# RWKV-7 layer of a hybrid decoder step: triangular inverses from transposed blocks by columns, samples' loads a pair ahead, masks and the second group's norm on VectorE, another gate for the first output half

## The chip, the cores and the metric

The kernel runs on one core of a Trainium2 chip. The metric is device time in microseconds (us), the time of one execution. In the profile PE is TensorE (matmul), PEld its weight loads, DVE VectorE, ACT ScalarE, POOL GpSimd and SP SyncE, which here only issues DMAs; ACT issues the loads of the weights beside its own work. Each engine works through its own instructions in order and waits at the first one whose operands or buffers are not ready.

## The reference, cut to what matters

One step of a two-layer decoder: 16 meta tokens and 512 prompt tokens, and 8 samples of 4 tokens each. Layer 0 is a gated DeltaNet mixer and a convolutional FFN, layer 1 an RWKV-7 mixer (16 heads of 64) and another FFN. All that follows concerns the RWKV mixer. Its core is a recurrence over tokens for each head:

```python
def rwkv_step(S, xs):
    r_t, w_t, k_t, v_t, kk_t, a_t = xs
    sa = jnp.einsum('bhvk,bhk->bhv', S, kk_t)
    S = (S * w_t[:, :, None, :] - sa[..., None] * (kk_t * a_t)[:, :, None, :]
         + v_t[..., None] * k_t[:, :, None, :])
    y = jnp.einsum('bhvk,bhk->bhv', S, r_t)
    return S, y
...
    kk = l2norm(heads(k * k_k))
...
    S, y = lax.scan(rwkv_step, S0.astype(F32), (tm(rh), tm(dh), tm(kh), tm(vh), tm(kk), tm(ah)))
    y = jnp.moveaxis(y, 0, 1)
    mu = jnp.mean(y, axis=-1, keepdims=True)
    var = jnp.mean(jnp.square(y - mu), axis=-1, keepdims=True)
    y = ((y - mu) * lax.rsqrt(var + GN_EPS)).reshape(B, L, D) * ln_w.astype(F32) + ln_b.astype(F32)
    bonus = jnp.sum(rh * kh * r_k.astype(F32), axis=-1, keepdims=True) * vh
    y = y + bonus.reshape(B, L, D)
    out = (y * gate.astype(F32)).astype(h.dtype) @ wo
```

The prompt's scan starts from zero states, the samples' from the given `state_rwkv_S`. Outputs are the activations and the new states.

## The kernel before, in words

All 560 tokens (32 of the samples, 16 meta, 512 of the prompt) lie along the free axis, features on the partitions. Every dense product in fp32 is made of three fp32r products: a weight tile is split into `hi` (on ACT, L70) and `lo` (on DVE, L71), the activations likewise, and `dense_g` (L115) runs hi·hi, hi·lo and lo·hi, two column halves each: 48 matmuls for a weight tile of 8 contraction blocks.

The scan is done in chunks: chunk 0 holds the samples and the meta tokens (48 columns), chunks 1 to 8 hold 64 prompt tokens each. Heads go in two groups G = 0, 1 of 8 heads, four pairs each. The steps for a group are generators that a small planner, `Weave`, interleaves: its `slots` hold the dense products of k, r and v, then the second group's `products2`, `gates` and `out_half`, in this order; its `chains` hold the others. A chain yields (PE cost, latency, banks), and the planner goes to whichever chain is due on its virtual clock, otherwise to the next dense matmuls. A slot may have a gate, a condition that must hold before it starts. The framework then schedules the instructions of each engine from a model of their times. The chains are:

- `sums` (L1298 and on): squares of k per head and token, their reciprocals `ssq` (upper partitions), the negatives `nw`.
- `early(G)` (from L1382): for each chunk the strictly triangular product of keys, `pa` in PSUM (L1392), times a mask on DVE (L1396) into an SBUF tile `L` of ring `s` (two buffers, shared with others); then eight ACT operations, one for each head, scale the rows by `ssq` (L1398); `to_inverse` stores the diagonal blocks (32 x 32; 16 x 16 for chunk 0) to DRAM on SP (L1373, L1378).
- `inverse0(G)` and `inverse(G)` load these blocks, one to a partition, into the tile `X` (24 partitions of 16 x 16 and 128 of 32 x 32), and `tri_inplace` inverts them in place on DVE, row by row from the last: a product (L1023) into the scratch tile `tri`, written across its rows, and a sum (L1025). The result goes to DRAM and from there into the chunks' tiles `A` (XX, A and A58 by name in the profile). Group 0's inverse runs beside the dense products of r and v, group 1's beside group 0's recurrence.
- `products(G, c)` (L1353, masks L1360): all key and query products of a chunk, whose corner blocks the inverses replace.
- `merge(G, q)` (L1439 to L1449): from the two inverted diagonal blocks of two chunks to the full 64 x 64 inverse. Four merges a group, one after the other.
- `ktokens`, `vtokens`: transposed keys and values by way of DRAM.
- `rec(G)` (L1594 to L1652): the serial chain over chunks. A chunk is four groups of matmuls, L1624 and L1628, L1633, L1642, L1651, each waiting for an evacuation of the one before. `load(c + 2)` on SP (L1572, L1573) fetches keys and values two chunks ahead. Group 1 starts when group 0 ends.
- `outnorm` (L1671 to L1691): the norm of two chunks' outputs: sum and mean on DVE, eight ACT operations that shift the heads (L1674), ACT square, DVE sum, inverse root in small DVE operations (L351 to L356), eight ACT operations that scale (L1681), four transpositions on PE (L1685), then gate and bonus on DVE (L1690, L1691).
- `samples(G)` (L1705 to L1761), four head pairs one after the other, sharing one set of buffers: `load(p)` issues 10 DMAs on SP (the states as block diagonals `S0b`, L1716 to L1717; `S0`, L1718; tokens, L1719 to L1724) and POOL places the queries in `z`; ten matmuls (L1738, L1739), two (L1744), two (L1749), on ACT eight masked copies `vm` (L1754), a matmul (L1757), and the new state through DVE (L1758) and POOL (L1759) to a store (L1760). When all four are done the samples have their own `outnorm`.
- `gates` (L1547): gate projection; `out_half` (from L1779): the first half, by contraction, of the output projection for all 8 output tiles (weights `w_o`, activations `osA`, built in a buffer that group 0's samples used), each stored to DRAM as `x2`. It starts when group 0's six norms and the gates are done and a merge of group 1 has been noted.

After the planner has run, the second half (`osB`) follows, adding `x2` (L1813), and then the FFN of layer 1.

## Time and profile before

| what | us |
|---|---|
| median of 3 runs (1908.01 to 1916.1) | 1912.06 |
| the profiled execution's own time | 1913.3 |
| its span in the profile | 1911.3 |
| PE busy / DVE busy / ACT busy / POOL busy | 1801.1 / 1154.5 / 803.9 / 369.0 |

The page of the profile gives the busy time of each engine, the clock that TensorE was granted in 40 slices (PEclk, in tenths of full speed), and the costliest groups of instructions: line, engine, operation, output <- input, count, then busy time, mean ns of one, and the idle time of the engine before them with what ended it. The view by windows gives the same for chosen stretches. A timeline row has start, length, engine, line, and in brackets the idle time just before with its releaser. The RWKV mixer runs from about 870 to 1480 us of the span. PE is busy for all 120 us between 1020 and 1140, where DVE is busy for 98.90; in 1190 to 1230 PE is busy for 28.55 of 40 us.

### The profile page before, as it was taken

The numbers are of one execution on the slowest core, as the hardware profiler recorded it, in microseconds if no ns is written. First come the engines' busy times: TensorE is split into PE (matmuls) and PEld (weight loads), VectorE is DVE, ScalarE is ACT, GpSimd is POOL, SyncE is SP. The second block draws the span as 40 slices with busy tenths as digits, with TensorE's granted clock in tenths as the row PEclk, the third lists the DMA queues.
The fourth block names the chain that finished last, engine by engine and source line by source line (L and its number), as shares of the span: only waits on it lengthen the run. The fifth ranks groups of instructions, "written<-read, shape, count | busy, mean of one in ns | idle before, by whom it ended". The sixth has DMA issues, their size and how long they took to land.

```text
span 1911.3 us, 36670 instructions
## 1 busy us (share of the span) xinstructions
PE 1801.1 (94%) x14673; PEld 1718.5 (90%) x14673; DVE 1154.5 (60%) x2221; ACT 803.9 (42%) x1779; POOL 369.0 (19%) x616
## 2 busy tenths in 40 slices
PE   7999999999999999998989999799997999999996
PEld 6889998789999999998778997788786999999996
DVE  6698973875555553337787977874555555554223
ACT  4766434442222222222976535554644322222221
POOL 3442403621222220013110000021001111111011
PEclk9999998999999999999898999896898999999998
DMA  4233232433222223444122244332235322223331
GB/s 131 76 91 93 70 90 104 150 122 120 82 89 89 80 87 104 120 155 98 48 70 62 70 117 121 98 91 80 78 102 163 123 89 89 89 88 91 99 109 67
DMA packets 128010, 186.13 MB, mean 97 GB/s; under 512 B 63088, under 2 KB 75376, under 8 KB 127840
## 3 DMA queue, kind: packets, MB, share of 16 engines
q10 hardware_dynamic: 34448, 111.63, 18.7%
q1 hardware_dynamic: 93392, 72.17, 13.0%
q8 instruction: 116, 1.90, 0.4%
q14 instruction: 54, 0.44, 0.1%
HBM read 151.56 MB, written 32.18 MB: 96 GB/s over the span
## 4 chain that ended last, share of the span: by engine, by line
PE 76%; DVE 12%; ACT 3%; DMA 3%; issue 1%; POOL 0%; SPq 0%; DVEq 0%; ACTq 0%
PE pd L115 56%; PE pd L138 3%; PE pg L1353 1%; DVE lo L71 1%; PE pg L1739 1%; PE pg L1628 1%; DVE it L425 1%; PE pg L1624 1%; PE pg L1651 1%; PE pg L1642 1%; DVE tri L1023 1%; PE pg L835 1%; PE pg L1633 1%; DVE cv L593 1%; DMA xd<-xo 1%
## 5 line engine op out<-in xcount | busy, mean ns | idle before, releaser
L115 PE MATMUL pd<-x,hi 128*128 128x280 f32 (+7 forms) x4768 | 837.5, 297 | 23.5 <-ACT hi L70 9.1
L115 PEld LDWEIGHTS pd<-x,hi 128*128 128x128 f32 (+1 forms) x4768 | 695.4, 192 | 30.8 <-ACT hi L70 9.3
L115 PE MATMUL pd<-x,lo 128*128 128x296 f32 (+5 forms) x2384 | 516.4, 297 | 5.6 <-DVE lo L71 5.6
L70 ACT ACTIVATE hi<-raw 128x1024 fp32r<-128x1024 f32 (+3 forms) x218 | 219.8, 1009 | 481.7 <-PE pd L115 447.4
L115 PEld LDWEIGHTS pd<-x,lo 128*128 128x128 f32 (+1 forms) x2384 | 382.9, 192 | 9.9 <-DVE lo L71 6.8
L71 DVE TENSOR_TENSOR lo<-raw,hi 128x1024 fp32r<-128x1024 f32 (+3 forms) x218 | 255.7, 1173 | 219.1 <-ACT hi L70 212.6
L218 POOL TENSOR_TENSOR s<-s,sq 128x560 f32<-128x560 f32 (+2 forms) x30 | 50.8, 1693 | 303.7 <-ACT sq L216 273.9
L304 DVE TENSOR_TENSOR gp<-pd,s 128x528 f32<-128x528 f32 (+1 forms) x44 | 30.8, 701 | 105.9 <-PE pd L115 105.9
L115 PE MATMUL pd<-hl,hi 128*128 128x280 f32 (+1 forms) x448 | 93.5, 290 | 0.0
L115 PE MATMUL pd<-hh,hi 128*128 128x280 f32 (+1 forms) x448 | 93.3, 290 | 0.0
L115 PE MATMUL pd<-hh,lo 128*128 128x280 f32 (+1 forms) x448 | 93.3, 290 | 0.0
L316 ACT ACTIVATE gs<-cv 128x528 f32<-128x528 f32 (+1 forms) x44 | 28.1, 639 | 147.3 <-DVE cv L314 147.3
L115 PE MATMUL pd<-hb,hi 128*128 128x280 f32 (+1 forms) x512 | 85.8, 290 | 0.0
L115 PEld LDWEIGHTS pd<-hb,hi 128*128 128x128 f32 x512 | 72.8, 188 | 0.0
L115 PEld LDWEIGHTS pd<-hh,lo 128*128 128x128 f32 x448 | 70.8, 188 | 0.0
L115 PEld LDWEIGHTS pd<-hh,hi 128*128 128x128 f32 x448 | 70.6, 188 | 0.0
L115 PEld LDWEIGHTS pd<-hl,hi 128*128 128x128 f32 x448 | 70.5, 188 | 0.0
L319 POOL TENSOR_TENSOR gs<-gs,s 128x560 f32<-128x560 f32 (+1 forms) x44 | 60.8, 1382 | 38.1 <-ACT gs L317 38.1
L322 DVE TENSOR_TENSOR h<-pd,gs 128x560 f32<-128x560 f32 (+1 forms) x44 | 32.1, 730 | 57.0 <-POOL gs L319 57.0
L308 POOL COPY fnew<-gp 128x2 f32<-128x2 f32 x44 | 8.1, 185 | 291.5 <-DVE gp L304 291.5
L1023 DVE TENSOR_TENSOR tri<-X 128x4 f32<-128x4 f32 (+26 forms) x124 | 56.0, 451 | 5.2 <-POOL X L1014 2.2
L138 PE MATMUL pd<-os,hi 128*128 128x280 f32 x256 | 52.8, 303 | 2.5 <-ACT os L183 1.9
(539 smaller groups left out, 3039.6 us busy)
## 6 DMA issues: line engine op xcount, KB each, us to landing
raw<-w_up ACTq DMA_DIRECT2D x88, 512.0 KB, 3.3
raw<-w_in ACTq DMA_DIRECT2D x32, 512.0 KB, 3.3
raw<-w_down ACTq DMA_DIRECT2D x32, 512.0 KB, 3.6
raw<-w_down ACTq DMA_DIRECT2D x16, 384.0 KB, 3.0
kbd<-kst SPq DMA_DIRECT2D x18, 256.0 KB, 2.0
KB<-kbd SPq DMA_DIRECT2D x18, 256.0 KB, 3.0
xd<-xo SPq DMA_DIRECT2D x16, 280.0 KB, 2.1
raw<-gdn_out ACTq DMA_DIRECT2D x8, 512.0 KB, 3.3
```

The lines of the kernel that those rows point to most:

```text
L70: nc.scalar.activation(hi[:R, :kt, :M], raw[:R, :kt, :M], AF.Copy)
L71: lo_eng.tensor_tensor(lo[:R, :kt, :M], raw[:R, :kt, :M], hi[:R, :kt, :M].bitcast(F32), op=ALU.subtract)
L115: nc.tensor.matmul(ps[b][:M, :c1 - c0] if isinstance(ps, list) else ps[:M, b, :c1 - c0], lhsT=w[:, kk, :M], rhs=x[:, c0:c1], start=(k == 0 ...
L138: nc.tensor.matmul(ps[:, b, :c1 - c0], lhsT=a, rhs=x[:, c0:c1], start=(k == i == 0), stop=(k == len(xs) - 1 and i == 2))
L218: nc.gpsimd.tensor_tensor(self.acc[:, :self.w], self.acc[:, :self.w], sq, op=ALU.add)
L304: nc.vector.tensor_tensor(two(gp[:, m0:]), pm, two(s[:, mo:mo + ml]), op=ALU.mult)
L316: nc.scalar.activation(gs[:, mo:mo + ml], cv[:, m0 - 2:], AF.Silu)
L319: nc.gpsimd.tensor_tensor(gs, gs, s[:, :n_main], op=ALU.mult)
L322: nc.vector.tensor_tensor(two(h), ps[:, :, :hw], two(gs), op=ALU.mult)
L425: nc.vector.tensor_tensor(t.rearrange("p n j -> p j n"), U[:n, i:R, c0:], L[:n, i, i:R].unsqueeze(2).to_broadcast([n, m, k]), op=ALU.mult)
L593: nc.vector.scalar_tensor_tensor(cv, gp[:, i:i + 584], cw[i], cv, op0=ALU.mult, op1=ALU.add)
L1023: nc.vector.tensor_tensor(t.rearrange("p n j -> p j n"), X[:n, i + 1:c1, c0:c1], X[:n, i, i + 1:c1].unsqueeze(2).to_broadcast([n, m1, k]), ...
```

## The change

1. `early` now computes the transposed blocks (operands of L1392 swapped, on the lower partitions, with a transposed mask `maskT` that one DMA puts into the free half of `nw`), and the eight ACT scalings of a chunk are gone. Instead `by_block(G, q)`, called from `sums`, copies the reciprocals on ACT into a tile of ring `s`, transposes them on PE, copies them on ACT and stores them to DRAM (`Dd`). `inverse` and `inverse0` load them as `D` (2 and 3 DMAs on SP) into `E.rest`, and DVE multiplies `X` by `D` once.
2. `tri_inplace` goes by columns: row j of `X` holds the block's column, the product is written along rows, the sums go down a column, and a DVE memset clears the used part of row j. For a 32 x 32 block that makes 43 products and sums and 31 memsets (before: 47 products and sums), for 16 x 16 it makes 15 and 15 (before: 15).
3. `samples`: the load is cut into three, each issued as soon as its buffers are free in the pair before. The eight ACT copies `vm` become one DVE product.
4. `outnorm` of group 1: shift and scale of the eight heads are one DVE operation each; group 0 keeps ACT's.
5. `out_half` no longer asks for a merge of group 1.

```diff
 def tri_inplace(E, X, tmp, n, R):
...
-    for i in range(R - 2, -1, -1):
-        m = R - 1 - i
-        step = min(m, N // m)
-        for c1 in range(R, i + 1, -step):
-            c0 = max(c1 - step, i + 1)
-            m1, k = c1 - i - 1, c1 - c0
-            t = tmp[:n, :m1 * k].rearrange("p (a b) -> p a b", a=k)
-            nc.vector.tensor_tensor(t.rearrange("p n j -> p j n"), X[:n, i + 1:c1, c0:c1],
-                                    X[:n, i, i + 1:c1].unsqueeze(2).to_broadcast([n, m1, k]), op=ALU.mult)
-            nc.vector.tensor_reduce(X[:n, i, c0:c1], t, axis=AX.X, op=ALU.add, negate=True)
+    for j in range(1, R):
+        i = 0
+        while i < j:
+            w = j - i
+            k = min(w, N // w)
+            t = tmp[:n, :k * w].rearrange("p (a b) -> p a b", a=k)
+            nc.vector.tensor_tensor(t, X[:n, i:i + k, i:j], X[:n, j, i:j].unsqueeze(1).to_broadcast([n, k, w]), op=ALU.mult)
+            nc.vector.tensor_reduce(X[:n, i:i + k, j], t, axis=AX.X, op=ALU.add, negate=True)
+            i += k
+        nc.vector.memset(X[:n, j, 0:j], 0.0)
         yield
...
+                by_block(m // 4, q)
                 W.chain(early(m // 4))
...
+        def by_block(G, q):
+            pt = bank([64])
+            s = E.xp.tile([P, T], F32, tag="s", name="Dt", bufs=2)
+            t = s[:72, :64]
+            nc.scalar.activation(s[up, 64:136].rearrange("p (c h) -> p c h", c=9), q, AF.Copy)
+            nc.tensor.transpose(pt[:72], s[up, 64:136], E.ident[up, up])
+            nc.scalar.activation(t, pt[:72], AF.Copy)
+            nc.sync.dma_start(out=Dd[G], in_=t)
...
-                        nc.tensor.matmul(pa[hh][up, u, :n], lhsT=KB[r, 4 * G + u, c, 1, :], rhs=KR[r, 4 * G + u, c, 1, :n], start=True, stop=True)
+                        nc.tensor.matmul(pa[hh][dn, u, :n], lhsT=KR[r, 4 * G + u, c, 1, :], rhs=KB[r, 4 * G + u, c, 1, :n], start=True, stop=True)
...
-                for h in range(8):
-                    nc.scalar.activation(L[:, h], L[:, h], AF.Copy, scale=ssq[up, c, 8 * G + h:8 * G + h + 1])
...
+            for j in range(2):
+                nc.sync.dma_start(out=D[64 * j:64 * j + 64], in_=Dd[G, 8:72, 32 * j:32 * j + 32])
+            nc.vector.tensor_tensor(X, X, D.unsqueeze(1).to_broadcast([P, 32, 32]), op=ALU.mult)
...
+            if G:
+                nc.vector.tensor_tensor(y, y, mu[r].unsqueeze(2).to_broadcast([r.stop - r.start, 8, 64]), op=ALU.add)
+            else:
+                for u in range(8):
+                    nc.scalar.activation(y[:, u], y[:, u], AF.Identity, bias=mu[r, u:u + 1])
...
-                for b8 in range(8):
-                    nc.scalar.activation(vm[:, b8], vx, AF.Copy, scale=ind[:, b8:b8 + 1])
+                nc.vector.tensor_tensor(vm, vx.unsqueeze(1).to_broadcast([P, 8, 64]), ind.unsqueeze(2).to_broadcast([P, 8, 64]), op=ALU.mult)
...
-                    [lambda: normed[0] == 6 and bool(gated) and bool(merged[1]), out_half()]]
+                    [lambda: normed[0] == 6 and bool(gated), out_half()]]
```

The loads of the samples, before and now (`load` and its three parts issue the same 10 DMAs; `load_states` also has the four POOL copies into `z`):

```diff
             for q in range(4):
                 p = 4 * G + q
-                load(p)
...
-                yield 0, 2.5, 0
...
                 nc.scalar.activation(PY, ps, AF.Copy)
+                if q < 3:
+                    load_states(p + 1)
...
                 nc.tensor.matmul(ps, lhsT=kt, rhs=vm, start=True, stop=True)
+                if q < 3:
+                    load_tokens(p + 1)
...
                 nc.sync.dma_start(out=O["rwkv_Ss"][p], in_=S0)
+                if q < 3:
+                    load_own(p + 1)
```

The change gives the planner other steps and other times, so instructions move on every engine. Two places matter for what follows. The first is DVE at the end of group 0's first large inverse (before: L1023 and L1025 its products and sums, L71 the split of a weight, 24 partitions the small inverse of group 1; L1439 is the first merge's transposition, which waits for the inverse's way through DRAM):

```order
L1023 TENSOR_TENSOR tri<-X 128x19x12
L1025 TENSOR_REDUCE X<-tri 128x12
L1023 TENSOR_TENSOR tri<-X 128x7x7
L71 TENSOR_TENSOR lo<-raw,hi 128x1024
L1025 TENSOR_REDUCE X<-tri 128x7
L71 TENSOR_TENSOR lo<-raw,hi 128x1024
L1023 TENSOR_TENSOR tri<-X 24x1
```

The same place now (L1379 is the mask of a chunk's products, L1537 to L1531 belong to `vtokens`, L1445 is the product of group 1's small blocks with D, L1462 the transposition):

```order
L1023 TENSOR_TENSOR tri<-X 128x361
L1379 TENSOR_TENSOR A<-pg,rc 128x4x128
L1024 TENSOR_REDUCE X<-tri 128x19
L1026 MEMSET X 128x31
L71 TENSOR_TENSOR lo<-raw,hi 128x1024
L1379 TENSOR_TENSOR A<-pg,rc 128x4x128
L1537 TENSOR_TENSOR H<-pg,H 128x280
L1528 TENSOR_TENSOR prod<-KR,KB 128x48
L1537 TENSOR_TENSOR H<-pg,H 128x280
L1529 TENSOR_TENSOR prod<-KR,KB 128x512
L1531 TENSOR_SCALAR brk<-rc,pv 128x128
L1445 TENSOR_TENSOR X<-X,rest 24x256
```

The inverse now ends ahead of work that stood before it: counted from the early products on, 11 weight splits stand ahead of its last row instead of 13, and 19 masks of products instead of 20. The second place is PE at the start of the first output half (before, in chunk 7 of group 1's recurrence: L1685 on XX is the norm of group 0's samples, L1744 and L1749 are steps of group 1's samples, L1642 and L1651 end chunk 7, L1624 and L1628 open chunk 8, `osA` is the output half):

```order
L1685 MATMUL pg<-cm,XX 128x32 x4
L1744 MATMUL pg<-A 32x64 x2
L1642 MATMUL pg<-KB 128x128 x4
L1651 MATMUL pg<-KB,A 64x64 x8
L115 MATMUL pd<-osA,hi 128x274 x2
L1624 MATMUL pg<-KB,KR 128x128 x4
L1628 MATMUL pg<-KB,A 64x64 x7
L1628 MATMUL pg<-KB,A 128x64
L1749 MATMUL pg<-A 32x64 x2
L115 MATMUL pd<-osA,hi 128x274 x5
```

The same now, in chunk 5 (the lines are in turn L1714, L1781, L1665, L1674, L1647, L1651 and L1786):

```order
L1714 MATMUL pg<-cm,XX 128x32 x4
L1781 MATMUL pg<-A 32x64 x2
L1665 MATMUL pg<-KB 128x128 x4
L1674 MATMUL pg<-KB,A 64x64 x6
L115 MATMUL pd<-osA,hi 128x274
L1674 MATMUL pg<-KB,A 64x64 x2
L115 MATMUL pd<-osA,hi 128x274 x5
L1647 MATMUL pg<-KB,KR 128x128 x4
L1651 MATMUL pg<-KB,A 64x64 x7
L1651 MATMUL pg<-KB,A 128x64
L1786 MATMUL pg<-A 32x64 x2
```

Both times the half comes right behind the norm of group 0's samples, but that norm now stands two chunks earlier in the recurrence, and the half's matmuls lie between the steps of chunks 5 to 8.

42 lines of the change are left out of this document (28 added, 14 removed).

## The prediction

> **What bounds the kernel now.** I read the page first: its engine table and the slices of the clock.
>
> ```profile
> span 1911.3 us, 36670 instructions
> PE 1801.1 (94%) x14673; PEld 1718.5 (90%) x14673; DVE 1154.5 (60%) x2221; ACT 803.9 (42%) x1779; POOL 369.0 (19%) x616
> PEclk9999998999999999999898999896898999999998
> ```
>
> PE is busy for 94% of the span, so only its 110 us of idle time and its time at a low clock can be won. Then I cut the RWKV layer, all that the change touches, into stretches with the view by windows (columns: length; busy time of PE, PEld, DVE, ACT, POOL; clock, DMA share, GB/s).
>
> ```profile
> 990.00:1020.00 30.00, 22.03 (x213) 20.80 (x212) 27.97 (x61) 22.49 (x70) 5.62 (x7) 0.72 0.20 49
> 1020.00:1140.00 120.00, 120.00 (x1025) 112.82 (x1024) 98.90 (x220) 55.95 (x150) 7.29 (x11) 0.99 0.32 92
> 1140.00:1190.00 50.00, 45.86 (x508) 39.90 (x507) 36.70 (x98) 27.20 (x61) 3.13 (x4) 0.90 0.48 125
> 1190.00:1230.00 40.00, 28.55 (x256) 24.31 (x254) 37.97 (x101) 21.50 (x68) 2.41 (x5) 0.87 0.26 78
> 1280.00:1300.00 20.00, 15.02 (x124) 12.86 (x123) 15.36 (x43) 15.38 (x45) 1.31 (x6) 0.91 0.31 79
> 1300.00:1340.00 40.00, 40.00 (x385) 34.73 (x382) 13.03 (x32) 18.19 (x56) 4.97 (x11) 0.57 0.27 77
> 1380.00:1400.00 20.00, 18.23 (x122) 15.55 (x122) 9.51 (x29) 11.29 (x39) 0.66 (x4) 0.66 0.13 36
> 1430.00:1450.00 20.00, 10.19 (x60) 8.06 (x60) 13.10 (x35) 10.34 (x32) 1.26 (x3) 0.88 0.56 165
> 1600.00:1700.00 100.00, 100.00 (x799) 100.00 (x798) 54.45 (x75) 30.00 (x42) 16.21 (x41) 1.00 0.26 85
> ```
>
> These are: the early products (PE idle 8.0); the first inverse under a full PE; the first merges; the first recurrence beside the second inverse (PE idle 11.5, DVE 95% busy); the gates (PE idle 5.0); the start of the second recurrence (no idle, clock 0.57); its chunks 6 and 7 (clock 0.66); its end (PE idle 9.8); and, for the price of a dense matmul, the last FFN: 100 us for 799, 0.125 us each.
>
> **The change part by part.** The sum is made against the profiled execution's own 1913.3 us (2.0 us beside its span); the median of the three runs, 1912.06, lies 1.2 lower.
>
> *Early products.* PE's waits there, and the group of the scalings on ACT that go:
>
> ```profile
> PE pg L1392 <- DVE L L1396: 2.5, 1, 2.5
> PE pg L1298 <- DVE L L1396: 2.4, 1, 2.4
> L1398 ACT ACTIVATE L<-L,ssq 64x64 f32<-64x64 f32 (+1 forms) x144 | 35.3, 328 | 9.0 <-DVE L L1396 6.8 <-issue 1.7 <-ACT L L1398 0.4
> ```
>
> A chunk's eight scalings stand between its masks and the store that frees L, 8 x 0.328 = 2.6 us. Without them the next masks get L sooner, and PE its bank. Of the two waits, 4.9 us, I take 4 as gone; what is late next is DVE, 27.97 of 30 busy. Against that stand two small transposes and, on SP, the loads of D, which are queued ahead of the stores of L and wait for D's own store. Bounds: 2 lost to 8 won (all idle time of this stretch).
>
> *The inverses.* DVE's rows for products of one size in the old form, for one element, and for plain rows:
>
> ```profile
> L1023 DVE TENSOR_TENSOR tri<-X 128x4 f32<-128x4 f32 (+26 forms) x124 | 56.0, 451 | 5.2 <-POOL X L1014 2.2
> L1023 DVE TENSOR_TENSOR tri<-X 128x375 f32<-128x375 f32 x1 | 0.8, 846 | 0.0
> L1023 DVE TENSOR_TENSOR tri<-X 128x1 f32<-128x1 f32 x2 | 0.3, 152 | 0.0
> L1025 DVE TENSOR_REDUCE X<-tri 128x1 f32<-128x1 f32 x2 | 0.3, 151 | 0.0
> L1506 DVE TENSOR_TENSOR prod<-KR,KB 128x512 f32<-128x512 f32 x2 | 1.4, 681 | 0.0
> L71 DVE TENSOR_TENSOR lo<-raw,hi 128x1024 fp32r<-128x1024 f32 x11 | 13.6, 1240 | 5.4 <-ACT hi L70 5.4
> ```
>
> The old products write their result across rows and cost (846 - 152) / 374 = 1.86 ns an element; the new ones write rows, and row L1506 gives (681 - 152) / 511 = 1.04. For one group of heads: 58 new products (43 + 15) over 8671 + 1240 elements, 58 x 0.152 + 9911 x 0.00104 = 19.1 us, against 56.0 / 2 = 28.0. The sums keep their elements (within 3%). New are 46 memsets, which no row shows: between 0 and the 0.151 us of a one-element sum, I take 0.1, 4.6 us; and the product with D, 1024 and 256 elements, 1.6 us. Net 2.7 us less on DVE per group (bounds: 7.3 less; 6.2 more if the new products cost the old rate). The Trainium skill, page "VectorE: DVE Perf Modes", section "Mode 1× (REGULAR) — the baseline", has fp32 with "weird strides" at one result per cycle like any other; by it the turn from columns to rows would win nothing per element, and the change would add 6.2 us. The trace disagrees, 1.86 against 1.04 ns, so I go by the rows, and keep 6.2 for a rival.
>
> What the shorter inverse does is decided by the order, shown with the change: on DVE the first inverse has moved up: 11 weight splits stand ahead of its last row instead of 13, and 3 instead of 4 ahead of its first. On PE 99 dense matmuls, 12.4 us, moved from before the first merge to behind it (89 stood between it and the first recurrence's chunk 1, 188 now); ahead of that chunk all work is as before. The trace at that place:
>
> ```profile
> 1131.23 0.20 DVE L1025 TENSOR_REDUCE X<-tri 128x7 f32<-128x49 f32 x1
> 1142.36 0.70 DVE L1439 STREAM_TRANSPOSE TY<-XX 32x512 f32<-32x512 f32 x1 [2.58 <-DMA XX<-UI]
> 1143.20 1.17 PE L1443 MATMUL pg<-TY,XX 32*32 32x32 f32 x32 [1.26 <-DVE TY L1439]
> ```
>
> So PE comes to the merge 12.4 us sooner, and the 11 us from 1131 to 1142 stay. DVE's last row comes sooner by 2.7 (cheaper), 2.5 (two splits of 1.24 later), 4 (early products) and perhaps 3 of the 6 us of one weight's matmuls (48 x 0.125), by which it starts sooner: 12. Then PE waits some 4 us more at the merge, and the 12.4 us behind it fill about 2 of the 4.1 us of idle time after it. Early products and first inverse together: -12 + 12.4 - 2, some 2 us won (9 won to 7 lost).
>
> *First recurrence.* Its PE work is the same chunk for chunk; where DVE is 95% busy, the second inverse is 2.7 us lighter: 3 won (0 to 6). *Gates*: samples' pairs now stand between them: 2 won of the 5.0 idle (0 to 4).
>
> *Samples, second norm, output half.* ACT loses a pair's eight masks and 16 operations of each norm in the second group:
>
> ```profile
> L1754 ACT ACTIVATE A<-A,rc 128x64 f32<-128x64 f32 x32 | 8.1, 334 | 0.1
> L1681 ACT ACTIVATE KB<-KB,gr 128x64 f32<-128x64 f32 x32 | 8.1, 335 | 7.5 <-DVE gm L1672 4.9 <-DVE gr L356 2.6
> L1758 DVE TENSOR_TENSOR A<-A,pg 128x512 f32<-128x512 f32 x4 | 2.7, 685 | 7.0 <-PE pg L1757 7.0
> ```
>
> Eight of 0.334 (2.7 us) become one DVE operation of 0.69; DVE has room there (18.19 of 40 is ACT, 13.03 DVE in the start of the second recurrence). With the loads split into three and issued as their buffers come free, SP no longer waits for a pair's end to load the next; its queue still holds the recurrence's loads behind each such wait, but those are two chunks ahead. So the first group's samples end sooner, and with them starts the output half. The order of PE shows it: the half starts two chunks sooner, in chunk 5 of the second recurrence instead of 7. In both orders it stands behind the samples' norm, so the gate's dropped condition was met already and costs nothing. Behind the last chunk stood 137 matmuls of the half, now 22: 14.4 us move ahead of it. The end, before:
>
> ```profile
> 1413.57 1.28 PE L1651 MATMUL pg<-KB,A 128*64 128x64 f32 x16
> 1434.55 0.27 PE L1685 MATMUL pg<-cm,KB 128*128 128x128 f32 x1
> 1447.63 0.31 PE L1685 MATMUL pg<-cm,A 32*128 32x32 f32 x1 [2.75 <-ACT A L1681]
> 1450.50 1.51 PE L115 MATMUL pd<-osB,hi 128*128 128x274 f32 x5 [1.12 <-ACT osB L183]
> ```
>
> ```profile
> 1419.31 0.73 DVE L1786 TENSOR_TENSOR xs<-pd,xs 128x548 f32<-128x548 f32 x1 [2.02 <-PE pd L115]
> 1423.19 0.73 DVE L1786 TENSOR_TENSOR xs<-pd,xs 128x548 f32<-128x548 f32 x1 [1.64 <-DMA xs<-xd]
> ```
>
> From the last chunk to the second half 35.7 us pass: the chunk's norm takes 20 to its transposition, behind additions that hold DVE's queue until PE or a load is done, and the samples' norm 13 more. Now the samples are nearly over and few additions are left: eight DVE operations of 0.69, some fifteen small ones and five hand-overs, about 12 us. So 23.7 won here; lost ahead of it 14.4 and a pair of samples, 2.6; won back there perhaps 3.3 of the time at clock 0.66. In all 10 (20 won; 3 lost if the norm still takes its 20 us). What then is late is the second half's own cycle of loads and stores, which stays.
>
> Sum: -2 - 3 - 2 - 10 = -17: 1896.3 beside 1913.3, and against the median 1895.
>
> **The rivals.** *The inverse is no shorter* (products at the old rate, 6.2 us more a group): its last row stays at 1131, the 12.4 us come on top, less 4 filled; the second inverse adds 4 beside the first recurrence; gates and end win 12. Together 0: 1912. For it: the memsets are unmeasured; against it: row L1506. Chance 0.17.
>
> *The end is not shorter*: additions still hold DVE, the norm takes 20 us, 3 lost instead of 10 won: 1908. For it, DVE now has the norm's products too. Chance 0.13.
>
> *Slower, by the clock at the first merge*: if the inverse is late by over 5 us more than I think, PE waits some 9 us and then runs merges and dense work at 0.57, as at 1300 to 1340, instead of 0.90: 45.9 x (0.90 / 0.57 - 1) = 27 us, 8 of wait, less 12: 1935. For it: after the 5.0 us idle of the gates PE stayed at 0.57 for 40 us though busy throughout. Against it: at 1190 to 1230 idle 11.5 us cost only 0.87. Chance 0.10. The Trainium skill, page "TensorE: Matmul & The Clock Gate", section "Part 1: The HAM clock gate", gives back the full clock after about 3.4 us of sustained work; by that such a wait would cost under 2 us more. The 40 us at 0.57 disagree.
>
> **How the numbers follow.** Forecast 0.60, the rivals 0.17, 0.13 and 0.10. About 0.5% (9.6 us) is what a measurement can tell from no change. Of the forecast 0.57 lie under 1902.5, of the first two rivals 0.05 more: faster 0.62; slower 0.13, the clock's 0.10 and 0.03 of the first; the rest, 0.25, is the same. The terms' bounds reach from -39 to +10 (1874 to 1922); all good or all bad at once is rare, so 1878 to 1914 leaves out the clock's 0.10 and about as much at the two ends.
>
> **What would show it.** Right: L's scalings gone and PE's wait on L under 1 us; new products near 0.54 us at 375 elements; PE's wait at the first merge under 6 us; osA under chunks 5 to 8; the second half starting within 15 us of the last chunk. Wrong: a long wait at the first merge with a clock under 0.7 behind it, or a last norm of 20 us.

## The result, and the profile after

The changed kernel takes 1901.49 us (median of 20 runs, 1890.89 to 1910.99), the kernel before 1912.09 us (20 runs, 1902.75 to 1924.47). The ratio is 0.9936, 95% interval 0.9918 to 0.9953: 12 us less by the ratio, within 9 and 16 (10.6 by the two medians). The forecast was 1895, 17 us less. The profiled execution has a span of 1894.0 us, which is below the median of its kernel; before it was 1911.3.

```profile
span 1894.0 us, 36463 instructions
PE 1791.6 (95%) x14675; PEld 1711.5 (90%) x14675; DVE 1153.9 (61%) x2321; ACT 731.3 (39%) x1479; POOL 369.9 (20%) x616
PEclk9999998999999999999897999797898899999998
```

ACT is 72.6 us less busy, DVE the same, and PE's idle time fell from 110 to 102 us. The view by windows, in the stretches that the prediction showed of before (length; PE, PEld, DVE, ACT, POOL; clock, DMA share, GB/s):

```profile
990.00:1020.00 30.00, 23.17 (x225) 21.89 (x223) 28.32 (x69) 9.47 (x15) 5.62 (x7) 0.72 0.22 53
1020.00:1140.00 120.00, 119.76 (x1096) 112.50 (x1095) 100.80 (x299) 39.38 (x74) 6.11 (x11) 0.99 0.35 98
1140.00:1190.00 50.00, 45.57 (x468) 40.87 (x467) 36.32 (x122) 27.74 (x67) 2.85 (x4) 0.93 0.43 120
1190.00:1230.00 40.00, 33.03 (x277) 28.81 (x276) 27.88 (x82) 20.25 (x66) 2.82 (x7) 0.79 0.32 96
1280.00:1300.00 20.00, 17.61 (x154) 15.09 (x153) 13.57 (x34) 11.22 (x29) 1.23 (x6) 0.74 0.36 93
1300.00:1340.00 40.00, 39.17 (x431) 32.34 (x428) 18.65 (x42) 11.65 (x28) 4.69 (x4) 0.74 0.23 70
1380.00:1400.00 20.00, 20.00 (x184) 18.80 (x183) 12.37 (x30) 6.08 (x15) 0.72 (x1) 1.00 0.67 184
1430.00:1450.00 20.00, 19.48 (x135) 19.45 (x136) 10.21 (x14) 8.48 (x14) 4.13 (x3) 0.86 0.52 153
```

The early products hardly gained: PE is busy for 23.17 of 30 us instead of 22.03, although ACT lost its scalings (22.49 to 9.47). PE's waits there are still the two on L, 4.4 us instead of 4.9, and the largest of the mixer are now at the end (L1714, the norm's transpositions):

```profile
PE pg L1714 <- DVE rsi L351: 8.6, 2, 6.8
PE pg L1714 <- ACT KB L1710: 6.6, 3, 2.4
PE pg L1411 <- DVE L L1415: 2.4, 1, 2.4
PE pg L1302 <- DVE L L1415: 2.0, 1, 2.0
```

The groups on DVE between 980 and 1290 us (busy, mean ns of one | idle time before, and what ended it) give the price of the inverse:

```profile
L1023 DVE TENSOR_TENSOR tri<-X 128x378 f32<-128x378 f32 (+26 forms) x116 | 38.7, 333 | 2.4
L1024 DVE TENSOR_REDUCE X<-tri 24x1 f32<-24x1 f32 (+28 forms) x116 | 37.9, 326 | 2.7
L1415 DVE TENSOR_TENSOR L<-pg,nw 64x256 f32<-64x256 f32 (+1 forms) x36 | 13.4, 402 | 3.7 <-DMA LI<-L 2.0 <-PE pg L1411 1.1 <-PE pd L115 0.5
L1026 DVE MEMSET X<- 24x1 f32 (+22 forms) x92 | 6.4, 70 | 0.0
L1426 DVE TENSOR_TENSOR X<-X,rest 128x1024 f32<-128x1024 f32 x2 | 2.5, 1226 | 3.9 <-DMA X<-LI 3.9
```

The products of both groups of heads take 38.7 us (38.2 were forecast, 56.0 before), the 92 memsets 6.4 instead of the 9.2 put down for them. Why the wait on L stayed is told by DVE's order around PE's two waits, which end at 1000.20 and 1004.78. After:

```profile
998.67 1.22 DVE L71 TENSOR_TENSOR lo<-raw,hi 128x1024 fp32r<-128x1024 f32 x1
999.81 1.27 DVE L1415 TENSOR_TENSOR L<-pg,nw 64x192 f32<-64x192 f32 x4
1004.31 1.08 DVE L1415 TENSOR_TENSOR L<-pg,nw 64x256 f32<-64x256 f32 x3 [0.51 <-DMA LI<-L]
```

and the second masks before:

```profile
1004.53 0.77 DVE L1396 TENSOR_TENSOR L<-pg,rc 64x256 f32<-64x256 f32 x2 [0.72 <-DMA LI<-L]
```

The first masks start without a pause behind other work of DVE, in both kernels. The second wait for the store of L (LI<-L), 0.51 us now and 0.72 before: the scalings, which stood ahead of the store, had cost two tenths there. The rest of both waits is DVE's own queue, which is busy for 28.32 of these 30 us. The first merge:

```profile
1115.97 0.52 DVE L1024 TENSOR_REDUCE X<-tri 128x19 f32<-128x361 f32 x1
1124.20 0.70 DVE L1462 STREAM_TRANSPOSE TY<-XX 32x512 f32<-32x512 f32 x1 [0.26 <-DMA XX<-UI]
1127.17 1.19 PE L1466 MATMUL pg<-TY,XX 32*32 32x32 f32 x32
```

The last sum ends at 1116.5 instead of 1131.4, and PE comes to the merge 16 us sooner and without a wait. The way through DRAM, from the last sum to the transposition, takes 7.7 us instead of the 11 that were to stay. And the end:

```profile
1411.99 1.28 PE L1674 MATMUL pg<-KB,A 128*64 128x64 f32 x16
1423.63 1.08 PE L1714 MATMUL pg<-cm,KB 128*128 128x128 f32 x4 [6.75 <-DVE rsi L351]
1426.89 0.82 PE L115 MATMUL pd<-osB,hi 128*128 128x274 f32 x2 [2.17 <-ACT osB L183]
1427.64 0.63 PE L1714 MATMUL pg<-cm,A 32*128 32x32 f32 x4
1430.53 1.51 PE L115 MATMUL pd<-osB,hi 128*128 128x274 f32 x5 [2.25 <-ACT osB L183]
```

From the last chunk (its end, 1413.3) 10.3 us pass to the norm's transpositions instead of 20, and 17.3 to the second half's steady run instead of 35.7.

To compare kernels whose orders differ, I cut each trace at marks that all have: the first early product, chunks 1 and 8 of the first recurrence, chunk 0 of the second, the end of its last chunk, the end of the second output half. Lengths in us from the timelines (the first column also carries what the clock does from 600 to 960 us, in code that no edit touches; and with the new inverse the first early product stands behind more dense products, so that this mark comes some 5 us later: the column less the clock lost in it is 952.6 on average there, 947.8 with the old inverse); in brackets what the records of the granted clock say was lost in the stretch (length times one minus the clock). The kernels below the second are the experiments.

| kernel | start to early | to chunk 1 | to chunk 8 | to second recurrence | to its last chunk (lost) | to end of second half |
|---|---|---|---|---|---|---|
| before | 975.6 | 211.7 | 79.0 | 34.5 | 114.1 (25.6) | 69.2 |
| after | 981.9 | 195.2 | 81.5 | 40.4 | 114.2 (11.9) | 46.7 |
| gate_back | 987.2 | 199.7 | 80.1 | 40.5 | 114.3 (11.9) | 51.6 |
| inv_only | 985.1 | 199.5 | 79.5 | 33.2 | 114.3 (25.6) | 66.7 |
| tail_only | 974.6 | 211.2 | 82.0 | 39.4 | 116.7 (15.4) | 50.6 |
| tail_noloads | 973.8 | 212.3 | 79.4 | 33.2 | 97.1 (5.1) | 64.8 |
| masks_only | 982.6 | 209.5 | 79.5 | 34.0 | 114.5 (22.9) | 74.6 |
| norm_only | 979.7 | 207.8 | 78.5 | 34.6 | 114.2 (27.3) | 61.3 |
| no_loads | 981.6 | 196.1 | 81.3 | 31.8 | 103.8 (11.9) | 65.3 |
| no_loads_2 | 979.7 | 198.4 | 81.7 | 31.8 | 103.9 (11.9) | 62.9 |
| no_norm | 980.0 | 197.1 | 81.4 | 40.5 | 120.2 (13.7) | 51.1 |
| hold4 | 986.2 | 197.7 | 81.4 | 40.3 | 109.4 (13.7) | 55.6 |
| fill_before | 979.8 | 207.8 | 78.5 | 34.6 | 130.7 (29.0) | 69.0 |

Ratios are to the kernel before on the same chip. The second table has, as means over all runs of a kernel, the span lost to the clock (span times one minus the granted clock of the run, so idle time at a low clock counts in it too) and what is left. One execution of the kernel before, 1996 us at a granted clock of 0.82, is left out as slow.

| kernel | ratio, 95% interval | runs | lost to the clock | span at full clock |
|---|---|---|---|---|
| before (four sets) | | 17 to 23 | 92.9 to 98.4 | 1814.3 to 1816.3 |
| after | 0.9936, 0.9918 to 0.9953 | 20 | 93.8 | 1804.6 |
| gate_back (order of after) | 0.9928, 0.9901 to 0.9956 | 12 | 91.1 | 1805.8 |
| inv_only | 0.9963, 0.9937 to 0.9989 | 12 | 94.3 | 1810.4 |
| tail_only | 0.9943, 0.9912 to 0.9973 | 9 | 92.7 | 1810.6 |
| tail_noloads | 0.9885, 0.9846 to 0.9924 | 6 | 70.5 | 1818.7 |
| masks_only | 0.9989, 0.9956 to 1.0023 | 12 | 86.3 | 1820.8 |
| norm_only | 0.9932, 0.9904 to 0.9960 | 12 | 85.7 | 1811.8 |
| no_loads | 0.9889, 0.9860 to 0.9917 | 5 | 81.0 | 1810.8 |
| no_loads_2 | 0.9909, 0.9873 to 0.9945 | 6 | 85.5 | 1807.3 |
| no_norm | 0.9954, 0.9928 to 0.9980 | 12 | 95.3 | 1806.7 |
| hold4 | 0.9915, 0.9886 to 0.9945 | 6 | 93.6 | 1804.4 |
| fill_before | 1.0075, 1.0045 to 1.0106 | 12 | 94.2 | 1831.3 |

### The profile page after: what moved, and what is told of

Read it like the earlier page. It is cut to its first block, busy times and chain, and to the rows that moved or that the text cites. A ratio compares the mean times of both kernels' runs of the same rounds, so it can differ in the third digit from the quotient of the medians.

```text
span 1894.0 us, 36463 instructions
## 1 busy us (share of the span) xinstructions
PE 1791.6 (95%) x14675; PEld 1711.5 (90%) x14675; DVE 1153.9 (61%) x2321; ACT 731.3 (39%) x1479; POOL 369.9 (20%) x616
## 4 chain that ended last, share of the span: by engine, by line
PE 79%; DVE 10%; ACT 3%; DMA 2%; issue 1%; SPq 0%; POOL 0%; ACTq 0%; DVEq 0%
PE pd L115 58%; PE pd L138 3%; PE pg L1372 1%; PE pg L1674 1%; PE pg L1774 1%; PE pg L1651 1%; PE pg L1665 1%; PE pg L1647 1%; PE pg L1656 1%; DMA xo<-x 1%; DVE lo L71 1%; PE pg L835 1%; PE pg L627 1%; PE pg L1793 1%; PE pg L1466 0%
## 5 line engine op out<-in xcount | busy, mean ns | idle before, releaser
L71 DVE TENSOR_TENSOR lo<-raw,hi 128x1024 fp32r<-128x1024 f32 (+3 forms) x218 | 253.5, 1163 | 219.8 <-ACT hi L70 213.0
L218 POOL TENSOR_TENSOR s<-s,sq 128x560 f32<-128x560 f32 (+2 forms) x30 | 50.6, 1685 | 309.1 <-ACT sq L216 278.8
L115 PEld LDWEIGHTS pd<-hl,hi 128*128 128x128 f32 x448 | 70.5, 188 | 0.0
L115 PEld LDWEIGHTS pd<-hh,hi 128*128 128x128 f32 x448 | 70.5, 188 | 0.0
L319 POOL TENSOR_TENSOR gs<-gs,s 128x560 f32<-128x560 f32 (+1 forms) x44 | 60.8, 1381 | 37.9 <-ACT gs L317 37.9
L115 PE MATMUL pd<-hb,lo 128*128 128x280 f32 (+1 forms) x256 | 53.3, 289 | 0.0
```

The costliest lines, as they stand in the source:

```text
L71: lo_eng.tensor_tensor(lo[:R, :kt, :M], raw[:R, :kt, :M], hi[:R, :kt, :M].bitcast(F32), op=ALU.subtract)
L115: nc.tensor.matmul(ps[b][:M, :c1 - c0] if isinstance(ps, list) else ps[:M, b, :c1 - c0], lhsT=w[:, kk, :M], rhs=x[:, c0:c1], start=(k == 0 ...
L218: nc.gpsimd.tensor_tensor(self.acc[:, :self.w], self.acc[:, :self.w], sq, op=ALU.add)
L319: nc.gpsimd.tensor_tensor(gs, gs, s[:, :n_main], op=ALU.mult)
```

## The experiments

### The two halves of the change, each alone

inv_only is the kernel before with parts 1 and 2 (diff of `early`, `by_block`, `inverse` and `tri_inplace` as above); tail_only has parts 3, 4 and 5.

> The kernel before with parts 1 and 2 of the change alone (transposed early products without scalings, D, inverse by columns); samples, second norm and gate as before. Theory (the gain has two separate sources, here and at the end): about 5 us of the 10.6 us are won by this half, ratio near 0.9975, 1907 us; the first merge about 15 us sooner than before, but the half of the output projection starts in chunk 7 and the way from the last chunk to the second half stays near 36 us. Rival A (all of the gain comes from the end; a shorter inverse only moves waits): ratio 1.000, 1912 us. Rival B (the inverse brings nearly all): 0.994, 1901 us.

> The kernel before with parts 3, 4 and 5 alone (samples' loads ahead, masks and second norm on VectorE, gate); inverses as before. Theory: some 6 us won, ratio near 0.997, 1906 us, with the first output half in chunk 5, about 20 of its 192 matmuls behind the last chunk and 15 us from the last chunk to the second half; the first merge at the time of before. Rival A (all of the gain from the end): ratio 0.994, 1901 us. Rival B (the inverse brings nearly all): 1.000, 1912 us.

Measured: 0.9963 and 0.9943, 7 and 11 us. Both halves win, as the theory said, and rivals A and B fall: neither carries all, though the end won what rival A had named, not the theory's 6 us. In inv_only the way from the early products to chunk 1 is 199.5 instead of 211.7 us (5 of these 12 are the first mark, as said above) and everything behind it is within 3 us of before; in tail_only it is 211.2, and the stretches from the first recurrence's end are those of the changed kernel. The sum of the halves, 18 us, is what was forecast for both; the changed kernel has 12 (9 to 16). The intervals are too wide to say that the halves take something from each other.

### Without the loads ahead

```diff
-                if q < 3:
-                    load_states(p + 1)
...
             for q in range(4):
                 p = 4 * G + q
+                load(p)
```

> The changed kernel with the samples' loads of before (each pair loaded when the last has ended), all else as changed. In the order the half then starts in chunk 7 again, with 143 of its matmuls behind the last chunk. Theory (what shortens the end is that the half is out of the way, which the loads bring): 6 us of the gain are lost, ratio near 0.9975, 1907 us, over 25 us from the last chunk to the second half. Rival (the norm on VectorE shortens the end by itself, and the 143 matmuls fill PE's wait there): ratio stays near 0.994, 1901 us, the way from the last chunk to the second half is 143 x 0.125 = 18 us of matmuls and under 5 us of idle time.

> The changed kernel with the samples' loads of before, a second time, beside the changed kernel's own order on the same chip. Theory (the loads ahead win about 6 us of time at full clock and lose about 13 us of clock: the first run had 81 us lost to the clock against 94): ratio 0.989 again, 0.986 to 0.992, span times granted clock about 1811 against 1805 us, and about 81 us lost to the clock. Rival (the first run's five executions fell well by chance): ratio 0.993 to 0.998, 90 us or more lost to the clock.

> The kernel before with only the masks and the second group's norm on VectorE and the gate's condition dropped; the inverses and the samples' loads as before (143 of the half's matmuls behind the last chunk). Theory (the loads ahead bring idle time back but cost clock, with the old inverse too): 8 to 12 us faster than before, ratio 0.994 to 0.996, no worse than with the loads ahead (0.9943). Rival (the loads ahead carry the gain of the end): ratio 0.997 to 1.000, 1906 to 1912 us.

Measured: 0.9889 and, repeated, 0.9909 with the new inverse, 0.9885 with the old one. Taking the loads ahead out makes the kernel no slower. By these ratios it is faster, by 9 us and, repeated, 4 beside the changed kernel, and by 11 beside tail_only; but the intervals touch or barely overlap in the first and the last case, and those of no_loads_2 and gate_back, which ran on one chip, overlap by more than half. The theory of no_loads fell, and with it a step of the prediction; the gain of tail_noloads is twice what its theory gave. That the loads ahead win at full clock and lose by the clock fits these means: 1810.8 us at full clock against the 1804.6 of the changed kernel and 81.0 us lost against 93.8; beside gate_back on one chip the same with smaller numbers, 1807.3 against 1805.8 and 85.5 against 91.1; 1818.7 against 1810.6 and 70.5 against 92.7 with the old inverse. What the loads do stands in the table of stretches. The last column falls by 15 us (64.8, 65.3, 62.9 to 46.7, 51.6, 50.6), since 123 matmuls of the half no longer stand there; the stretch with the second recurrence grows by 14 (97.1, 103.8, 103.9 to 114.2, 114.3, 116.7), where they stand now; and the stretch ahead of it grows by 8 (about 32 to 40). The last is the price. The samples' matmuls over the states between chunk 8 of the first recurrence and the second recurrence, after:

```profile
1264.25 1.83 PE L1774 MATMUL pg<-XX 128*128 128x128 f32 x14
1277.75 1.73 PE L1774 MATMUL pg<-XX 128*128 128x128 f32 x14
1296.54 1.83 PE L1774 MATMUL pg<-A 128*128 128x128 f32 x14
```

and before, where the second recurrence starts at 1300.8:

```profile
1277.91 1.83 PE L1739 MATMUL pg<-XX 128*128 128x128 f32 x14
```

Three pairs of samples instead of one are worked off ahead of the serial chain that sets the end. What they leave behind is filled with the half's matmuls, and the three stretches together get no shorter.

### Which of masks and norm

masks_only and norm_only are the kernel before with one edit each; no_norm is the changed kernel with the second group's norm back on ScalarE.

```diff
-                for b8 in range(8):
-                    nc.scalar.activation(vm[:, b8], vx, AF.Copy, scale=ind[:, b8:b8 + 1])
+                nc.vector.tensor_tensor(vm, vx.unsqueeze(1).to_broadcast([P, 8, 64]), ind.unsqueeze(2).to_broadcast([P, 8, 64]), op=ALU.mult)
```

```diff
-            for u in range(8):
-                nc.scalar.activation(y[:, u], y[:, u], AF.Identity, bias=mu[r, u:u + 1])
+            nc.vector.tensor_tensor(y, y, mu[r].unsqueeze(2).to_broadcast([r.stop - r.start, 8, 64]), op=ALU.add)
```

> The kernel before with one edit: the samples' eight masked copies on ScalarE become one product on VectorE. Theory (these copies hold ScalarE's queue while the second recurrence starts, so that PE's matmuls come too thin and the clock stays at one half; without them it does not): most of the 22 us that masks and norm win together, ratio 0.990 to 0.994, 1893 to 1901 us, span lost to the clock near 80 us against 94, and a granted clock over 0.8 in 1300 to 1340 us instead of 0.57. Rival (the second norm on VectorE wins it): ratio 0.997 to 1.000, 1906 to 1912 us, the clock as before.

> The kernel before with one edit: the second group's norm shifts and scales on VectorE (two products instead of 16 operations of 0.33 us on ScalarE, five times). Masks and norm together, without the loads ahead, took 0.9885; the masks alone 0.9989. Theory (the norm carries it: ScalarE's evacuations in the second recurrence no longer stand behind the norm's operations): ratio 0.987 to 0.993, 1887 to 1898 us, and a granted clock over 0.8 in 1300 to 1340 us. Rival (only both together free ScalarE enough in the stretch where the clock stays at one half): ratio 0.995 to 1.000, 1902 to 1912 us, and a clock under 0.7 there.

> The changed kernel with the second group's norm on ScalarE as before, loads ahead and masks as changed. In the order none of the half's 192 matmuls stands behind the last chunk. Theory (the early half, not the norm's engine, shortens the end; 16 ScalarE operations of 0.33 us come back, half of them ahead of the transposition of the last norm): 2 to 5 us slower than the changed kernel, ratio 0.995 to 0.9965, 1904 to 1907 us, and 5 us more of idle PE time behind the last chunk. Rival (VectorE's queue is what the last norm waits for, and ScalarE is free): as fast as the changed kernel or faster, ratio 0.990 to 0.994.

Measured: 0.9989 for the masks, 0.9932 for the norm, 0.9885 for both; without the norm on VectorE the changed kernel is at 0.9954. So the theory of masks_only fell and the norm carries more: at full clock the masks alone lose 5 us (1820.8 against 1815.8 on their chip), the norm alone wins 4 (1811.8 against 1816.2). no_norm lies where its theory put it (PE idles 11.9 us between last chunk and second half instead of 8.9, where 5 more were expected), though its interval reaches into the rival's. tail_noloads also drops the gate's condition; that changes nothing there, for the half starts in chunk 7, and a chunk of group 1 can only be planned when a merge of group 1 has been noted. norm_only landed between its two lines: its time is near the theory's, its clock is the rival's. The clock in 1300 to 1340 us, where the second recurrence starts; tail_noloads, which has both edits:

```profile
1300.00:1340.00 40.00, 37.90 (x499) 32.64 (x499) 21.52 (x50) 13.86 (x34) 4.97 (x11) 0.98 0.31 89
```

norm_only:

```profile
1300.00:1340.00 40.00, 40.00 (x357) 34.57 (x353) 11.97 (x27) 13.80 (x40) 4.97 (x11) 0.51 0.23 66
```

masks_only:

```profile
1300.00:1340.00 40.00, 38.84 (x389) 33.31 (x390) 16.61 (x34) 14.20 (x37) 5.36 (x11) 0.59 0.26 73
```

With both, PE does 499 matmuls in these 40 us at a clock of 0.98; with one of them 357 and 389 at 0.51 and 0.59, in norm_only without an idle moment. These three are single executions, and those of masks_only and norm_only are the ones of their 12 that lost most to the clock (106 and 99 us of span). Without the loads ahead, the five traces that lack one of the edits or both lose 22.9 to 29.0 us of clock in the second recurrence and, fill_before aside, take 114 us for it; the three that have both lose 5.1 to 11.9 and take 97 to 104.

Over all runs the picture is less sharp. The span lost to the clock is 82 to 113 us in the runs of the kernel before, 72 to 106 with the masks alone, 72 to 99 with the norm alone, and 62 to 80 in the six runs with both. So each edit alone wins some 7 or 8 us of clock on average, and both together 23. That one edit alone never ends the low clock is not shown.

### Is it too little work that keeps the clock down?

fill_before adds matmuls whose results are overwritten by the next ones, ahead of the second and third group of chunks 1 to 4:

```diff
                 ps2 = bank([4, P])
+                if G and 1 <= c <= 4:
+                    w = KR[:, 4:8, c].rearrange("p u a b -> p u (a b)")
+                    for _ in range(2):
+                        nc.tensor.matmul(ps2, lhsT=w[:, 0], rhs=w, start=True, stop=True)
```

> The kernel before with 16 matmuls more whose results are overwritten: two of 128 x 128 by 512 columns ahead of the second and the third matmul group of chunks 1 to 4 of the second recurrence, 0.56 us each by the samples' last matmuls of that size, so 9 us of work more if none of it lies in waits. Theory (the clock halves when the matmuls of a stretch fill the array too little, even without idle time): the stretch 1300 to 1340 runs at a clock over 0.8 instead of 0.57, the span lost to the clock falls by 8 us or more from 94, and the time stays within 5 us of before or falls, ratio 0.994 to 1.002. Rival (the clock there follows from idle time just before, and more work cannot bring it back): clock 0.5 to 0.6 as before and the work adds 9 us at full or 18 at half speed, ratio 1.004 to 1.010, 1920 to 1931 us.

Measured: 1.0075, and the clock of 1300 to 1340 us as before:

```profile
1300.00:1340.00 40.00, 40.00 (x345) 31.73 (x342) 10.69 (x26) 14.94 (x44) 4.98 (x11) 0.57 0.22 61
```

These are the rival's numbers, but the edit hardly reaches the stretch that it was to test. The clock falls to one half at 1300.9 us, and the first added matmul (L1635) runs at 1331.7, since chunk 1 comes late in the stretch. fill_before:

```profile
1301.00:1331.00 30.00, 30.00 (x253) 25.69 (x251) 5.95 (x11) 11.43 (x33) 3.27 (x10) 0.50 0.23 61
1331.69 3.61 PE L1635 MATMUL pg<-KR 128*128 128x512 f32 x4
1335.00:1341.00 6.00, 6.00 (x70) 4.40 (x70) 2.51 (x12) 2.13 (x7) 0.00 (x0) 1.00 0.19 54
1337.88 1.98 PE L1648 MATMUL pg<-KR 128*128 128x512 f32 x4
```

norm_only, whose trace is alike up to 1331 us and which has no added matmuls:

```profile
1301.00:1331.00 30.00, 30.00 (x253) 25.63 (x250) 6.62 (x12) 9.37 (x25) 3.23 (x10) 0.50 0.22 61
1335.00:1341.00 6.00, 6.00 (x41) 5.31 (x39) 2.90 (x11) 4.39 (x15) 0.00 (x0) 0.50 0.30 95
```

A matmul in fp32 makes two records, so two of the 16 added ones lie at the low clock. Right behind them, at 1335.0, the clock is 1.00 and stays there to 1393, past the last of them; in norm_only it stays at 0.50 until 1341.8. So this run does not show that more work cannot bring the clock back; this one place speaks for the theory. What the run does show is that the added work wins nothing: over its 12 runs 94.2 us are lost to the clock as before (94.0), and 15.5 us more are needed at full clock, 0.97 for each matmul (by the row of L1648, 0.99; the 0.56 that was expected is one record's).

The 14 traces (those of the table and that of prices, below) allow a closer look. The records of the granted clock hold only 1.0 and 0.5, in stretches that are whole multiples of 3.41 us (but for the last of a trace). For each such window I add up the work of the matmuls that start in it: columns, at 0.46 ns each in the dense fp32r products (0.125 us for 272) and at twice that for a record in fp32, times the share of the 128 rows that the contraction fills. Then I ask for the clock of the next window:

| work in a window | at full clock | of these, next at half | at half clock | of these, next at half |
|---|---|---|---|---|
| under 1.2 us | 224 | 223 | 311 | 308 |
| 1.2 to 1.6 us | 162 | 88 | 188 | 127 |
| over 1.6 us | 6615 | 17 | 258 | 8 |

A limit of 1.46 us tells the next clock in all but 105 of 7758 windows. PE's busy time, at its best limit, leaves 487 wrong, and the work without the share of rows 303. So in these traces it is too little work in a window that goes with the low clock, whether PE is busy or not. norm_only falls to one half behind a window with 70 matmuls and 0.65 us of work: two groups of 32 merge matmuls of 32 x 32, which fill a quarter of the rows. In tail_noloads a window's edge lies between the same two groups, the two windows have 1.18 and 1.77 us, and the clock stays (the first of them is one of the 105). In fill_before the window with the first added matmuls has 1.88 us and ends the low stretch; without them norm_only has 0.67 there. This is a reading of the traces, not a run of its own; only that last pair varies the work alone.

### The gate, and one order twice

gate_back restores `bool(merged[1])` in the gate.

> The changed kernel with the dropped condition of the gate put back. Every engine's order of instructions is the same as in the changed kernel, so this measures the changed kernel once more. Theory (the condition was met already and costs nothing): ratio 0.9936 within the interval of the changed kernel, 0.992 to 0.995. Rival (chips or hours differ by more than the intervals say): outside of it.

Measured: 0.9928, as the theory said. This pair of traces is worth more than the gate: the order is the same on every engine, the profiled executions differ by 7.6 us. In 860 to 960 us, which no edit of this study touches, after:

```profile
860.00:960.00 100.00, 90.57 (x620) 81.19 (x619) 75.08 (x115) 62.77 (x109) 23.30 (x38) 0.91 0.27 72
```

and gate_back:

```profile
860.00:960.00 100.00, 92.48 (x591) 81.24 (x590) 71.41 (x108) 56.95 (x101) 21.55 (x37) 0.85 0.26 73
```

The same instructions get a clock of 0.91 or 0.85, and 29 matmuls fewer are done by 960 us. So the 17.3 us between the first two profiles are not the gain, however close to the forecast's 17, and single traces are compared by stretches only.

### The half held back

hold4 lets blocks 4 to 7 of the first output half depend on chunk 8, so that 73 of its matmuls instead of 20 stand behind the last chunk, where PE idled 11.2 us:

```diff
+                if m == 4:
+                    while not last:
+                        yield 0.1
...
+                    nc.gpsimd.tensor_scalar(hz, Pt[:, 0, 0:8], 0.0, None, op0=ALU.mult)
+                    nc.gpsimd.tensor_tensor(cols, cols.bitcast(F32), hz.unsqueeze(2).to_broadcast([P, 8, 2]), op=ALU.add)
```

> The changed kernel, where blocks 4 to 7 of the first output half wait until chunk 8 has begun (two small GpSimd operations add zero times a value of chunk 8 to two columns of the half's activations): 73 instead of 20 of the half's matmuls stand behind the last chunk. Theory (PE's 11.2 us idle behind the last chunk are the next bound, and the half's matmuls fit there): 53 x 0.125 = 6.6 us move into the idle time, about 5 us faster than the changed kernel, ratio near 0.991, 1896 us. Rival (chunks 5 to 8 then wait where the matmuls lay, or the held blocks' additions hold up the norm on VectorE): no gain or a loss, ratio 0.994 to 0.998, 1901 to 1908 us.

Measured: 0.9915, 2 to 4 us better than the changed kernel's two values, which both lie in its interval: not clear. The ratio is the one that the theory named, but the trace speaks for the rival:

```profile
1425.05 0.42 PE L115 MATMUL pd<-osA,lo 128*128 128x274 f32 x2
1432.11 1.12 PE L1718 MATMUL pg<-cm,KB 128*128 128x128 f32 x4 [6.65 <-DVE KB L1711]
```

The held matmuls do run right behind the last chunk (end 1415.1), but the norm's transpositions come 17.0 us behind it instead of 10.3, after an idle time of 6.65 us as before: the idle time moved with the work.

### The price of writing across rows

prices has 73 operations more behind the last output; four forms of a product and two of a sum, four times each:

```diff
+                nc.vector.tensor_tensor(t, xin, outer, op=ALU.mult)
+                nc.vector.tensor_tensor(t, xin, inner, op=ALU.mult)
+                nc.vector.tensor_tensor(tT, xin, outer, op=ALU.mult)
+                nc.vector.tensor_tensor(tT, xin, inner, op=ALU.mult)
+                nc.vector.tensor_reduce(px[:, 960:960 + a], t, axis=AX.X, op=ALU.add)
+                nc.vector.tensor_reduce(px[:, 960:960 + a], tT, axis=AX.X, op=ALU.add)
```

> The changed kernel with 73 VectorE operations more behind the last output: products of 15 x 25, 4 x 25 and 25 x 15 elements on 128 partitions, in four forms (result along rows or across rows; the broadcast operand constant along the rows or across them), and sums of both layouts. Theory (writing across rows costs): 0.84 us for 375 elements across rows and 0.54 along rows, whichever way the broadcast lies; a sum read across rows costs as one read along them. Rival (the operand that is constant along the inner loop costs): 0.84 us with it and 0.54 without, whichever way the result is written.

The groups (L2066 to L2071 in the order of the diff; `t` lies along rows, `tT` across them):

```profile
L2068 DVE TENSOR_TENSOR pt<-px 128x375 f32<-128x375 f32 x8 | 6.5, 812 | 0.2
L2069 DVE TENSOR_TENSOR pt<-px 128x375 f32<-128x375 f32 x8 | 6.4, 803 | 0.3
L2066 DVE TENSOR_TENSOR pt<-px 128x375 f32<-128x375 f32 x8 | 4.4, 548 | 0.2
L2067 DVE TENSOR_TENSOR pt<-px 128x375 f32<-128x375 f32 x8 | 4.4, 547 | 0.2
L2071 DVE TENSOR_REDUCE px<-pt 128x25 f32<-128x375 f32 x4 | 3.2, 805 | 0.1
L2070 DVE TENSOR_REDUCE px<-pt 128x25 f32<-128x375 f32 x4 | 2.2, 545 | 0.1
...
L2066 DVE TENSOR_TENSOR pt<-px 128x100 f32<-128x100 f32 x4 | 1.4, 341 | 0.1
L2068 DVE TENSOR_TENSOR pt<-px 128x100 f32<-128x100 f32 x4 | 1.3, 333 | 0.1
```

For 375 elements it is 0.80 to 0.81 us across rows and 0.55 along them, whichever way the broadcast lies: the theory holds for the products, the rival falls. (The first of the 100-element products along rows, 0.58 us, was the first of its shape; the other three took 0.26, against 0.33 across rows.) In one point the theory was wrong: a sum that reads across rows pays the same, 0.805 against 0.545.

## Why the prediction was right, point by point

The time lies in the range, the sign and the likeliest case were right, the size was 17 us against 12 (9 to 16). The terms were less right than their sum: some came larger, some with the other sign, and that they nearly cancel was luck.

*Early products, 4 won.* The step failed: PE's wait on L was to fall under 1 us and fell from 4.9 to 4.4. The scalings cost 0.2 us of it; what PE waited for is DVE's own queue, which the forecast had named as the next limit.

*Inverses.* The prices were right: 0.548 us for 375 elements, 38.7 us of products against 38.2, and per group DVE wins (56.0 + 38.5 - 38.7 - 37.9 - 6.4 - 3.3) / 2 = 4.1 us instead of 2.7 (38.5 were the sums before; 3.3 are both products with D). The Trainium skill, page "VectorE: DVE Perf Modes", section "Mode 1× (REGULAR) — the baseline", has fp32 with odd strides at one result per cycle like any other. The experiment on prices disagrees: 375 elements cost nearly half as much again, read or written across rows.

*Early products and first inverse together, 2 won.* Mis-sized. Over the six traces with the old inverse chunk 1 of the first recurrence starts at 977.7 + 210.0 = 1187.7 on average, over the seven with the new one at 983.1 + 197.7 = 1180.8: 7 won, inside the bounds (9 won to 7 lost), with single traces from 1185.8 to 1192.1 and from 1177.0 to 1186.9. The forecast had PE wait 4 us more at the first merge, because 99 dense matmuls no longer stand ahead of it. But in this pair the last row came 15 us sooner, not 12, and the merge has no wait at all. From its first product to its last sum the inverse takes 72.7 to 73.4 us in the seven traces, 84.1 to 84.3 in the six: 11 us less, where cheaper operations and two splits were to give 5. The way through DRAM is 3 us shorter as well, and against that the inverse starts only 2 us sooner on average, not 7. Where the rest of the 11 us comes from stays open. Behind the merge the clock stays at 1.00 until 1179 us, where it fell to 0.69 at 1145 before.

*First recurrence, 3 won.* Nothing was won: 81.0 us on average with the new inverse (79.5 to 81.7), 79.5 with the old (78.5 to 82.0). PE's clock fell there (0.79 instead of 0.87 in 1190 to 1230), though PE was idle for 7.0 us instead of 11.5.

*Gates, 2 won.* With the loads ahead this stretch is 5 to 6 us longer than before, since it holds three pairs of samples instead of one; without them it is 1 to 3 us shorter.

*The end, 10 won.* The size was right (tail_only: 11, 5 to 17), and so were the marks: the half under chunks 5 to 8, the second half 13.6 us behind the last chunk with its first matmul and 17.3 with the rest. From the last chunk to the second half's steady run 18.4 us were won, where 23.7 were forecast. The reason was half wrong. Ahead of that 17 us of work were to come in and 3.3 of low clock to go; in the second recurrence the clock gave back 13.7 (25.6 lost before, 11.9 after), so that with the half's matmuls in it it is as long as before. The forecast let the loads ahead bring the gain, by an earlier half, and gave masks and norm ScalarE's 2.7 us a pair. The runs point the other way: masks and norm alone win 22 us (15 to 29), all of it as clock (23.4 us less lost, 2.4 more needed at full clock), and by the ratios the loads ahead give some of it back.

*Rivals.* "The inverse is no shorter" and "the end is not shorter" did not come. "Slower, by the clock at the first merge" did not come there; but the stretch from which it took its price, 1300 to 1340 at 0.57, is where much of the gain at the end arises, and the forecast had only said "no idle" of it and looked for its gain elsewhere. That a dropped condition costs nothing was right.

Why the clock stays at one half there the traces tell as far as PE goes: too little work in a window, as worked out under fill_before. It is shown that both edits together lower the lost clock, in all six runs of tail_noloads; each alone does so by a third of that on average. That ScalarE's operations are what thins out PE's work is only argued. The Trainium skill, page "TensorE: Matmul & The Clock Gate", section "Part 1: The HAM clock gate", has the full clock back after about 3.4 us of sustained work; norm_only, busy by the profile's count for all of 40 us at 0.51, disagrees. The same section has the clock vary from run to run by where its free-running window falls; the pair of traces with one order agrees, with 7.6 us between the two, and the runs of the two kernels with this order lose from 77 to 103 us to the clock.

## What to carry to other kernels

Cost the stretches in which PE is busy at a low clock like idle time: here 94 us were lost to the clock, nearly as much as PE idled, and the version with the lowest ratio (masks and norm alone, 0.9885) won by the clock alone, with no time won at full clock (1818.7 against 1816.3). Look there for windows full of small matmuls: PE counts as busy in them, and the clock falls behind them. Before an experiment on such a stretch is believed, look whether its edit runs inside it. Work that is started early because its data is there is no gain when a serial chain behind it sets the end: look at what it stands ahead of. And before two traces are compared, compare two of the same order: in this kernel they differ by 7.6 us where nothing was changed.

## What the runs showed of the hardware

- VectorE in fp32: products of 375 elements 0.55 us along rows, 0.81 with the result written across rows; sums 0.545 and 0.805 by the way they read. A broadcast operand costs nothing in either direction. Memsets of 1 to 31 elements a row take 0.07 us on average.
- TensorE's granted clock was 1.0 or 0.5, in windows of 3.41 us. The same instructions had a mean clock of 0.91 and 0.85 in 860 to 960 us of two executions; 1300 to 1340 us ran at 0.98 in tail_noloads and at 0.51 to 0.59 in the five kernels that lack one or both of its edits on masks and norm and load as before.
- In 7758 windows of 14 traces the next window's clock followed the work done (columns at their full-clock price times the share of rows filled): at half in 531 of 535 behind less than 1.2 us, at full in 6848 of 6873 behind more than 1.6 us. PE busy throughout was not enough: 30 us at 0.50 in norm_only.
- An fp32 matmul of 128 x 128 by 512 columns cost 0.99 us at full clock and 1.8 at half.
